# Splitting the returned columns of a feed-forward block two groups later, and starting its down projection with two units for one block of tokens

## The chip, the cores and the metric

The kernel runs on one core of one Trainium2 chip. The metric is device time in microseconds (us) of one execution. An execution with the hardware profiler on leaves a trace; times inside it are counted from the first instruction (its "span").

## The reference, cut to what matters

Two layers of a decoder trunk work on 256 tokens of width 1024. Each layer begins and ends with a feed-forward block, and the change touches only these (four of them in all):

```python
def swiglu(x, w_gu, w_down):                      # x 256 x 1024, w_gu 1024 x 5632, w_down 2816 x 1024
    gate, up = jnp.split(x @ w_gu, 2, axis=-1)
    return (jax.nn.silu(gate) * up) @ w_down
...
h = layer_norm(DEEPNORM_ALPHA * x + 0.5 * swiglu(x, ffn1_w_gu, ffn1_w_down), ln_g[0], ln_b[0])
... # three token mixers side by side, gated and projected, layer norm
return layer_norm(DEEPNORM_ALPHA * h + 0.5 * swiglu(h, ffn2_w_gu, ffn2_w_down), ln_g[2], ln_b[2])
```

## The kernel before, in words

**Weights.** All weights come as one stream of units of 128 x 1024 fp32 (512 KB). `unit` (L99) loads a unit into a buffer `raw` by a DMA from the SP queue (L110), and `split` (L115) makes two fp32r tiles of it: `whi`, a cast on ACT (L116), and `wlo`, the rest, a subtraction on DVE (L117). There are three `raw` buffers and five each of `whi` and `wlo`. Activations are split in the same way, by the same two lines. `mm3` (L131) multiplies two split operands with three matmuls (L126).

**Gate and up.** A feed-forward block has eleven groups (0 to 10) of 256 gate and 256 up columns. A group takes four units; for each of eight slices of the width and each of two blocks of 128 tokens (tb 0 and 1) three matmuls of 512 columns are issued, 48 in all. A group fills two of the four `acc` banks of PSUM, one per block. The loop is in `rest` (L357); group 0 is done by `first` or `both`.

**Out and back.** `out` (L330) takes a finished group. Per block ACT applies Silu from PSUM into a tile `t` (L336) and DVE multiplies by the up half (L337), which frees the bank. DVE transposes 32 x 32 squares, `t` into `z` (L340). Four DMAs from the POOL queue write `z` into a DRAM tile `tr` (L344), and a fifth brings it back in the order of a full transpose into `y` (L345). `t`, `z` and `y` share one tag of four buffers, `t2` (the trace calls all three `t`). Later `settle` (L348) splits `y` into `u0` to `u10` (lines 116 and 117 once more, `u<-t`), the operands of the down projection. Each call of `out` for group i first multiplies, then settles group i-1, then transposes group i.

**Down.** `projA` (L173) multiplies the 22 slices of `u` with 22 units. The sums of block 0 are two banks `a`, `b`, those of block 1 are `c`, `d` and a half bank `at` (`full_rows`, L216). `c` and `d` are the banks that group 10 used, so they are free only after its two multiplications on DVE. Unit 0 is done for block 0, then for block 1, then unit 1, and so on. After unit 8 the last group is settled (`along`). The last four or six units (`tail`) are kept to the end.

**What sets the order.** Each engine takes its instructions in one fixed order. A planner lays that order down when the program is built: on every engine it takes next what its own cost estimates say is ready, and of several ready ones the first in the program; loads and splits of weight units count as 300 instructions earlier than they stand (`AHEAD`, L100). `tc.issue_after(ins)` keeps what is traced inside it behind `ins`, but only on the engine of `ins`. In `settle` that is DVE, so the subtraction is held behind the multiplication of the newer group, and the cast on ACT is not held by anything but its operand.

Of the kernel before, what the change touches and what calls it, by code (L numbers as in the profile page):

```python
# [17 lines left out]
P = 128  # L18
D = 1024
# [3 lines left out]
NFT = FF // P  # L23
# [13 lines left out]

@with_exitstack
def tile_trunk(ctx, tc, x, xT, mem, memT_, wst, lnp, memln, cvw, rows, cst, out):
    nc = tc.nc  # L40
    pc = ctx.enter_context(tc.tile_pool(name="pc", bufs=1))
# [4 lines left out]
    p2 = ctx.enter_context(tc.tile_pool(name="p2", bufs=2))  # L46
# [7 lines left out]
    def nm(s):  # L54
        uid[0] += 1
        return f"{s}_{uid[0]}"

    def T(pool, shape, tag, dt=F32, bufs=None):
        kw = {} if bufs is None else {"bufs": bufs}
        return pool.tile(shape, dt, tag=tag, name=nm(tag), **kw)  # L60

    def acc():
        return T(psA, [P, 512], "acc")
# [30 lines left out]
        nc.scalar.copy(t.rearrange("p v k -> p (v k)"), zero.to_broadcast([P, 2 * S]))  # L94


    pos, newest = [0], [None]

    def unit(w=U, dst=None, cuts=1, behind=None):  # L99
        ahead = tc.high_priority(offset=AHEAD) if pos[0] >= 8 * P * U else nullcontext()  # L100
        raw = T(praw, [P, U], "raw")
        src = wst[pos[0]:pos[0] + P * w].rearrange("(p w) -> p w", p=P)
        pos[0] += P * w
        (ph, th), (pl, tl) = dst or ((phi, "whi"), (plo, "wlo"))
        with ahead:
            hi = T(ph, [P, U], th, F32R)
            lo = T(pl, [P, U], tl, F32R)
            for i in range(cuts):
                c = slice(i * w // cuts, (i + 1) * w // cuts)
                nc.sync.dma_start(raw[:, c], src[:, c])  # L110
                with tc.issue_after(behind) if behind else nullcontext():
                    newest[0] = split(hi[:, c], lo[:, c], raw[:, c])
        return hi, lo

    def split(hi, lo, src):  # L115
        nc.scalar.copy(hi, src)  # L116
        return nc.vector.tensor_tensor(lo, src, hi.bitcast(F32), op=ALU.subtract).ins  # L117
# [3 lines left out]
    def pe(ins):  # L121

        return tc.keep_in_program_order(ins) if pinned[0] else ins

    def matmul(*a, **k):
        return pe(nc.tensor.matmul(*a, **k))  # L126
# [4 lines left out]
    def mm3(o, l, r, first, last, skip=False):  # L131
        (lh, ll), (rh, rl) = l, r
        matmul(o, lh, rh, start=first, stop=False, skip_group_check=skip)
        matmul(o, lh, rl, start=False, stop=False, skip_group_check=skip)
        matmul(o, ll, rh, start=False, stop=last, skip_group_check=skip)

    def weave(work, steps):

# [34 lines left out]
    def projA(xt, w, kpu, nk, outs, tail=0, dsts=(), lead=0, after=None, behind=None, held=(), led=None, along=None):  # L173

        def one(k, kk, hi, lo, tb, j):
            ts = slice(tb * P, (tb + 1) * P)
            n = [o.shape[-1] for o in outs[tb]]
            c = kk * w + sum(n[:j])
            c = slice(c, c + n[j])
            mm3(outs[tb][j], (xt[0](k)[:, ts], xt[1](k)[:, ts]), (hi[:, c], lo[:, c]), k == 0, k == nk - 1)  # L180

        nu = nk // kpu
        units = {}

        def get(uu):
            if uu not in units:
                t = uu - (nu - tail)
                units[uu] = unit(kpu * w, dsts[t] if 0 <= t < len(dsts) else None, behind=behind if uu in held else None)
            return units[uu]

        def run(us, tb, js):
            for uu in us:
                for kk in range(kpu):
                    for j in js:
                        one(uu * kpu + kk, kk, *get(uu), tb, j)

        for tb in range(2):
            run(range(lead), tb, range(len(outs[tb])))
            if led:
                led(tb)  # L200
        for uu in range(lead, nu - tail):
            for tb in range(2):
                run([uu], tb, range(len(outs[tb])))
            if along and uu == 8:
                along(newest[0])
        for uu in range(nu - tail, nu):
            get(uu)
        turns = ()
        for tb in range(2):
            for j in range(len(outs[tb])):  # L210
                run(range(nu - tail, nu), tb, [j])
                if j and turns:
                    turns.pop(0)()
            turns = after and after(tb, outs)

    def full_rows():  # L216

        a, b, c, d = (acc() for _ in range(4))
        return [[a, b], [c, d[:, 0:S], at()[:, 0:S]]]
# [72 lines left out]
    class Ffn:  # L292
        def __init__(self, before=None):
            self.units = []
            for q in range(KD // 2):
                if before:
                    before(q)
                self.units.append(unit(cuts=2 if before and q == 0 else 1))
            self.hu, self.bank, self.due = {}, {}, None

        def h(self, i):
            if i not in self.hu:
# [17 lines left out]
        def both(self, hT):  # L320
            self.bank = {tb: acc() for tb in range(2)}
            for k in range(KD):
                hi, lo = self.units[k // 2]
                c = slice((k % 2) * 512, (k % 2) * 512 + 512)
                for tb in range(2):
                    ts = slice(tb * P, (tb + 1) * P)
                    mm3(self.bank[tb], (hT[0][:, k, ts], hT[1][:, k, ts]), (hi[:, c], lo[:, c]), k == 0, k == KD - 1)
            self.out(0, self.bank)

        def out(self, i, banks):  # L330


            t = T(p2, [P, 8, 2, 32], "t2", bufs=4)
            for tb in range(2):
                g, u = (banks[tb][:, c:c + S].rearrange("p (j x) -> p j x", j=8) for c in (0, S))
                nc.scalar.activation(t[:, :, tb, :], g, AF.Silu)  # L336
                ins = nc.vector.tensor_tensor(t[:, :, tb, :], t[:, :, tb, :], u, op=ALU.mult).ins  # L337
            self.settle(ins)
            z = T(p2, [P, 512], "t2", bufs=4)
            nc.vector.transpose(z, t.rearrange("p j t x -> p (j t x)"))  # L340
            y = T(p2, [P, 512], "t2", bufs=4)
            d = T(pd, [4, 32, 4, P], "tr")
            for q in range(4):
                nc.gpsimd.dma_start(d[:, :, q].rearrange("b c x -> c b x"), z[32 * q:32 * q + 32].rearrange("c (b x) -> c b x", b=4))  # L344
            nc.gpsimd.dma_start(y, d.rearrange("b c q x -> (b c) (q x)"))  # L345
            self.due = (i, y)

        def settle(self, behind):  # L348

            if self.due:  # L350
                (i, y), self.due = self.due, None
                hi, lo = (self.h(i)[:, n].rearrange("p a (t q s) -> p (a t) q s", t=2, q=4) for n in range(2))
                with tc.issue_after(behind):
                    split(hi, lo, y.rearrange("p (q n s) -> p n q s", q=4, n=4))
            self.last = behind

        def rest(self, hT, tail, dsts, post, mid={}, behind=None):  # L357
            for i in range(1, NFT // 2):
                banks = [acc() for _ in range(2)]
                for uu in range(KD // 2):  # L360
                    hi, lo = unit(behind=behind if i == 1 and uu < 2 else None)
                    for kk in range(2):
                        k, c = 2 * uu + kk, slice(kk * 512, kk * 512 + 512)
                        for tb in range(2):
                            ts = slice(tb * P, (tb + 1) * P)
                            mm3(banks[tb], (hT[0][:, k, ts], hT[1][:, k, ts]), (hi[:, c], lo[:, c]), k == 0, k == KD - 1)
                self.out(i, banks)
                for f in (2 * i, 2 * i + 1):
                    if f in mid:
                        with tc.issue_after(self.last):  # L370
                            mid[f]()
            outs = full_rows()
            projA((lambda k: self.hu[k // 2][:, 0, k % 2, :], lambda k: self.hu[k // 2][:, 1, k % 2, :]), D, 1, NFT, outs, tail, dsts, after=post, along=self.settle)

    class Post:

# [106 lines left out]
    def mixers(l, hT, mkT, mv_, post):  # L483
        xt = acc_of(hT)
        pinned[0] = True

        outs = [[acc()[:, :MOD // 2] for _ in range(2)] for _ in range(2)]
        projA(xt, MOD, 1, KD, outs, 3)
        ba = T(pu, [P, 2, 8], "ba")
        zs = T(pu, [P, 2, 512], "u3")  # L490
# [544 lines left out]
    for l in range(NL):  # L1035
# [4 lines left out]
        post = Post(lnp[l, 0, 0], lnp[l, 0, 1])  # L1040
# [9 lines left out]
        last = l == NL - 1  # L1050
        post = Post(lnp[l, 2, 0], lnp[l, 2, 1], last)
# [92 lines left out]
```

## Time and profile before

| what | value |
|---|---|
| three timed runs | 1354.88, 1358.7 and 1361.22 us, median 1358.7 us |
| the profiled execution | 1357.15 us, of which the span is 1355.4 us |
| matmuls, PE busy | 7160, 96% of the span |
| DVE, ACT, POOL busy | 62%, 48%, 15% of the span |
| DMA, mean over the span | 194 GB/s |
| granted TensorE clock, mean | 0.98 |

PE is TensorE's matmuls, PEld its weight loads, DVE is VectorE, ACT is ScalarE, POOL is GpSimd; SP issues the DMAs of the weight stream. Ends of matmuls are modelled, so neighbours overlap in the table of times and a PE that is "busy" need not be at its peak. In the views, `u<-t L116 ACT` is the cast of columns that came back, `u<-t,u L117 DVE` the subtraction, `t<-t L340` the transposition, `tr<-t L344` and `t<-tr L345` the way out to DRAM and back. A wait "A <- B: 10.0, 4, 3.0" says that A sat idle for 10.0 us before 4 of its instructions until B ended, 3.0 us at the longest. The two layers' feed-forward blocks lie at about 0 to 200, 490 to 690, 690 to 865 and 1155 to 1355 us.

### The profile page before, as it was taken

The page shows a single profiled execution, that of the slowest core. Times are in us where ns is not written, and L with a number is a line of the kernel's source. Part 1 is how long each engine was busy: PE and PEld are TensorE (multiplying, and loading weights), DVE is VectorE, ACT ScalarE, POOL GpSimd, SP SyncE. Part 2 cuts the span into 40 slices and gives each one's busy share as a digit, 9 for nine tenths or more (in the row PEclk, how much of TensorE's full clock was granted, in tenths as well). Part 3 has the DMA queues.
Part 4 walks back from the last instruction along what each step waited for, and adds up shares of the span by engine and source line. Part 5 has one row for each costly group of instructions (what it writes and reads, how often), then busy time and mean ns, then how long its engine had stood idle before and what let it go on. Part 6 is the DMA issues. An engine that isn't in the chain of part 4 may idle for free.

```text
span 1355.4 us, 19229 instructions
## 1 busy us (share of the span) xinstructions
PE 1294.4 (96%) x7160; PEld 1097.7 (81%) x7160; DVE 845.7 (62%) x1266; ACT 654.6 (48%) x979; POOL 197.8 (15%) x357
## 2 busy tenths in 40 slices
PE   8998799999999999998999989999999999999797
PEld 6876688999878788776888867899987788887686
DVE  5575557697556776455575554668867378654555
ACT  6443444566574544333444443446656644443441
POOL 0222200102301002121012220001024100121200
PEclk9998899999999999998999998999999999999899
DMA  8876774654644747666867666646554266666663
GB/s 266 290 241 198 244 235 144 203 182 135 155 137 136 233 131 226 218 207 190 261 206 242 209 213 214 215 147 211 172 138 147 91 189 199 196 207 219 219 200 110
DMA packets 77982, 263.54 MB, mean 194 GB/s; under 512 B 11872, under 2 KB 13024, under 8 KB 77888
## 3 DMA queue, kind: packets, MB, share of 16 engines
q1 hardware_dynamic: 66320, 232.53, 53.7%
q0 software_dynamic: 11568, 29.77, 7.6%
q8 instruction: 56, 0.92, 0.3%
q14 instruction: 38, 0.31, 0.1%
HBM read 247.45 MB, written 14.81 MB: 193 GB/s over the span
## 4 chain that ended last, share of the span: by engine, by line
PE 50%; DMA 27%; DVE 8%; issue 6%; ACT 6%; POOL 3%; SPq 0%; POOLq 0%; DVEq 0%; ACTq 0%
PE acc L126 40%; DMA t<-tr 9%; DMA raw<-in_wst_dram 9%; DMA tr<-t 9%; PE at L126 4%; DVE wlo L117 3%; POOL tr L344 3%; ACT whi L116 3%; PE sm L126 3%; ACT u L116 2%; DVE t L340 2%; PE sm L129 1%; DMA ms<-mst 1%; DVE u L117 1%; PE at L129 0%
## 5 line engine op out<-in xcount | busy, mean ns | idle before, releaser
L117 DVE TENSOR_TENSOR wlo<-raw,whi 128x1024 fp32r<-128x1024 f32 (+2 forms) x403 | 479.8, 1207 | 306.4 <-ACT whi L116 304.0
L116 ACT CAST whi<-raw 128x1024 fp32r<-128x1024 f32 (+2 forms) x403 | 409.2, 1034 | 404.8 <-DMA raw<-in_wst_dram 233.8
L126 PE MATMUL acc<-whi,hT 128*128 128x512 f32 (+1 forms) x1824 | 572.0, 391 | 15.1 <-ACT whi L116 15.1
L126 PEld LDWEIGHTS acc<-whi,hT 128*128 128x128 f32 x1824 | 345.2, 191 | 87.7 <-ACT whi L116 18.4
L126 PE MATMUL acc<-wlo,hT 128*128 128x512 f32 (+1 forms) x912 | 355.9, 390 | 8.9 <-DVE wlo L117 8.9
L126 PE MATMUL acc<-whi,u 128*128 128x512 f32 (+1 forms) x800 | 257.6, 386 | 24.0 <-DVE t L337 24.0
L126 PEld LDWEIGHTS acc<-wlo,hT 128*128 128x128 f32 x912 | 173.9, 191 | 46.7 <-DVE wlo L117 14.0
L126 PEld LDWEIGHTS acc<-whi,u 128*128 128x128 f32 x800 | 154.7, 195 | 57.2 <-DVE t L337 19.0
L344 POOL DMA_DIRECT2D tr<-t x176 | 96.2, 553 | 399.1 <-DVE t L340 385.6
L126 PE MATMUL acc<-wlo,u 128*128 128x512 f32 (+1 forms) x400 | 153.2, 383 | 0.0
L126 PE MATMUL acc<-hT,whi 128*128 128x256 f32 x672 | 122.3, 284 | 0.0
L126 PEld LDWEIGHTS acc<-hT,whi 128*128 128x128 f32 x672 | 104.7, 192 | 0.0
L117 DVE TENSOR_TENSOR u<-t,u 128x512 fp32r<-128x512 f32 x44 | 30.4, 692 | 113.7 <-ACT u L116 113.7
L116 ACT CAST u<-t 128x512 fp32r<-128x512 f32 x44 | 27.3, 620 | 144.8 <-DMA t<-tr 144.8
L126 PE MATMUL acc<-hT,wlo 128*128 128x256 f32 x336 | 95.1, 283 | 0.0
L126 PEld LDWEIGHTS acc<-wlo,u 128*128 128x128 f32 x400 | 78.2, 196 | 14.2 <-DVE wlo L117 0.3
L126 PEld LDWEIGHTS acc<-hT,wlo 128*128 128x128 f32 x336 | 64.4, 192 | 0.0
L345 POOL DMA_DIRECT2D t<-tr x44 | 24.6, 559 | 192.7 <-DMA tr<-t 140.0
L126 PE MATMUL at<-whi,u 128*128 128x256 f32 x152 | 39.8, 287 | 0.0
L337 DVE TENSOR_TENSOR t<-t,acc 128x256 f32<-128x256 f32 x88 | 36.0, 414 | 3.4 <-ACT t L336 3.3
L512 DVE SCALAR_TENSOR_TENSOR t<-acc,cw,t 128x255 f32<-128x255 f32 (+2 forms) x72 | 34.5, 479 | 0.9
L126 PE MATMUL acc<-whi,w 128*128 128x512 f32 (+1 forms) x96 | 31.0, 392 | 2.7 <-DVE w L117 2.7
(249 smaller groups left out, 1264.7 us busy)
## 6 DMA issues: line engine op xcount, KB each, us to landing
raw<-in_wst_dram SPq DMA_DIRECT2D x409, 512.0 KB, 4.4
tr<-t POOLq DMA_DIRECT2D x176, 64.0 KB, 3.9
t<-tr POOLq DMA_DIRECT2D x44, 256.0 KB, 3.5
raw<-in_wst_dram SPq DMA_DIRECT2D x16, 324.0 KB, 2.9
gB<-in_lnp_dram SPq DMA_DIRECT2D x6, 512.0 KB, 6.1
bB<-in_lnp_dram SPq DMA_DIRECT2D x6, 512.0 KB, 6.0
mdr<-w POOLq DMA_DIRECT2D x4, 512.0 KB, 6.8
w<-dr POOLq DMA_DIRECT2D x4, 512.0 KB, 12.3
```

Of the source, the lines that this page charges most:

```text
L116: nc.scalar.copy(hi, src)
L117: return nc.vector.tensor_tensor(lo, src, hi.bitcast(F32), op=ALU.subtract).ins
L126: return pe(nc.tensor.matmul(*a, **k))
L129: return pe(nc.tensor.transpose(*a))
L337: ins = nc.vector.tensor_tensor(t[:, :, tb, :], t[:, :, tb, :], u, op=ALU.mult).ins
L340: nc.vector.transpose(z, t.rearrange("p j t x -> p (j t x)"))
L344: nc.gpsimd.dma_start(d[:, :, q].rearrange("b c x -> c b x"), z[32 * q:32 * q + 32].rearrange("c (b x) -> c b x", b=4))
L345: nc.gpsimd.dma_start(y, d.rearrange("b c q x -> (b c) (q x)"))
L512: nc.vector.scalar_tensor_tensor(yc[:, j, d:], b[:, j, :S - d], w[:, t:t + 1], yc[:, j, d:], op0=ALU.mult, op1=ALU.add)
```

## The change

Settling is put off: `out` keeps a list of groups that are on their way, and when it has transposed group i it settles group i-2, if there is one, with the subtraction held behind the transposition instead of the multiplication. `y` moves to a tag with two buffers, `pt`, which the feed-forward blocks did not use. Two groups are left for the down projection, settled after its units 2 and 5; what is handed to `issue_after` there is now a matmul, an instruction of PE, so it holds nothing on ACT or DVE. And the down projection begins with `lead` 2: units 0 and 1 for block 0, then units 0 and 1 for block 1, then the others as before.

```diff
     def unit(w=U, dst=None, cuts=1, behind=None):
...
                 with tc.issue_after(behind) if behind else nullcontext():
-                    newest[0] = split(hi[:, c], lo[:, c], raw[:, c])
+                    split(hi[:, c], lo[:, c], raw[:, c])
...
     def mm3(o, l, r, first, last, skip=False):
...
-        matmul(o, ll, rh, start=False, stop=last, skip_group_check=skip)
+        return matmul(o, ll, rh, start=False, stop=last, skip_group_check=skip).ins
...
         for tb in range(2):
-            run(range(lead), tb, range(len(outs[tb])))
+            if lead:
+                run(range(lead), tb, range(len(outs[tb])))
             if led:
                 led(tb)
         for uu in range(lead, nu - tail):
             for tb in range(2):
-                run([uu], tb, range(len(outs[tb])))
-            if along and uu == 8:
-                along(newest[0])
+                ins = run([uu], tb, range(len(outs[tb])))
+            if along and uu in (2, 5):
+                along(ins)
...
-            self.hu, self.bank, self.due = {}, {}, None
+            self.hu, self.bank, self.due = {}, {}, []
...
                 ins = nc.vector.tensor_tensor(t[:, :, tb, :], t[:, :, tb, :], u, op=ALU.mult).ins
-            self.settle(ins)
+            self.last = ins
             z = T(p2, [P, 512], "t2", bufs=4)
-            nc.vector.transpose(z, t.rearrange("p j t x -> p (j t x)"))
-            y = T(p2, [P, 512], "t2", bufs=4)
+            ins = nc.vector.transpose(z, t.rearrange("p j t x -> p (j t x)")).ins
+            if len(self.due) > 1:
+                self.settle(ins)
+            y = T(p2, [P, D], "pt")[:, 0:512]
...
-            self.due = (i, y)
+            self.due.append((i, y))
...
             if self.due:
-                (i, y), self.due = self.due, None
+                i, y = self.due.pop(0)
                 hi, lo = (self.h(i)[:, n].rearrange("p a (t q s) -> p (a t) q s", t=2, q=4) for n in range(2))
                 with tc.issue_after(behind):
                     split(hi, lo, y.rearrange("p (q n s) -> p n q s", q=4, n=4))
-            self.last = behind
...
-            projA(..., D, 1, NFT, outs, tail, dsts, after=post, along=self.settle)
+            projA(..., D, 1, NFT, outs, tail, dsts, 2, post, along=self.settle)
```

More of the change, by code (lines that the diff above doesn't have):

```diff
@@ L94, in tile_trunk @@
         nc.scalar.copy(t.rearrange("p v k -> p (v k)"), zero.to_broadcast([P, 2 * S]))
-    pos, newest = [0], [None]
+    pos = [0]
     def unit(w=U, dst=None, cuts=1, behind=None):
@@ L179, in one @@
             c = slice(c, c + n[j])
-            mm3(outs[tb][j], (xt[0](k)[:, ts], xt[1](k)[:, ts]), (hi[:, c], lo[:, c]), k == 0, k == nk - 1)
+            return mm3(outs[tb][j], (xt[0](k)[:, ts], xt[1](k)[:, ts]), (hi[:, c], lo[:, c]), k == 0, k == nk - 1)
         nu = nk // kpu
@@ L191, in run @@
         def run(us, tb, js):
+            ins = None
             for uu in us:
@@ L194, in run @@
                     for j in js:
-                        one(uu * kpu + kk, kk, *get(uu), tb, j)
+                        ins = one(uu * kpu + kk, kk, *get(uu), tb, j)
+            return ins
         for tb in range(2):
-            run(range(lead), tb, range(len(outs[tb])))
+            if lead:
+                run(range(lead), tb, range(len(outs[tb])))
             if led:
@@ L372, in rest @@
             outs = full_rows()
-            projA((lambda k: self.hu[k // 2][:, 0, k % 2, :], lambda k: self.hu[k // 2][:, 1, k % 2, :]), D, 1, NFT, outs, tail, dsts, after=post, along=self.settle)
+            projA((lambda k: self.hu[k // 2][:, 0, k % 2, :], lambda k: self.hu[k // 2][:, 1, k % 2, :]), D, 1, NFT, outs, tail, dsts, 2, post, along=self.settle)
     class Post:
```

## The prediction

> **What bounds the kernel now.** I read the page first, then the waits, then the busy time by stretch, then the timeline of one group on each engine.
>
> ```profile
> span 1355.4 us, 19229 instructions
> ...
> PE 50%; DMA 27%; DVE 8%; issue 6%; ACT 6%; POOL 3%; SPq 0%; POOLq 0%; DVEq 0%; ACTq 0%
> PE acc L126 40%; DMA t<-tr 9%; DMA raw<-in_wst_dram 9%; DMA tr<-t 9%; PE at L126 4%; DVE wlo L117 3%; POOL tr L344 3%; ACT whi L116 3%; PE sm L126 3%; ACT u L116 2%; DVE t L340 2%; PE sm L129 1%; DMA ms<-mst 1%; DVE u L117 1%; PE at L129 0%
> ```
>
> The chain that ended last is half PE, but 18% of it is the way of the columns to DRAM and back, in a kernel whose PE looks 96% busy. The waits say who stands still for that way:
>
> ```profile
> ACT u L116 <- DMA t<-tr: 144.8, 43, 7.0
> ...
> DVE u L117 <- ACT u L116: 120.8, 49, 6.4
> ```
>
> All but one of the 44 casts wait for their columns, 3.4 us each (144.8 / 43), and DVE stands behind them. One turn of it, in layer 1's first block, groups 9 and 10, first ACT, then DVE, then POOL:
>
> ```profile
> 808.61 0.62 ACT L116 CAST u<-t 128x512 fp32r<-128x512 f32 x1 [2.88 <-DMA t<-tr]
> 809.14 2.96 ACT L116 CAST whi<-raw 128x1024 fp32r<-128x1024 f32 x3
> 812.00 0.38 ACT L336 ACTIVATE t<-acc 128x256 f32<-128x256 f32 x1
> 816.06 1.04 ACT L116 CAST whi<-raw 128x1024 fp32r<-128x1024 f32 x1 [3.69 <-DMA raw<-in_wst_dram]
> 817.01 0.38 ACT L336 ACTIVATE t<-acc 128x256 f32<-128x256 f32 x1
> 820.26 0.62 ACT L116 CAST u<-t 128x512 fp32r<-128x512 f32 x1 [2.87 <-DMA t<-tr]
> ```
>
> ```profile
> 809.87 0.71 DVE L340 STREAM_TRANSPOSE t<-t 128x512 f32<-128x512 f32 x1
> ...
> 813.87 0.41 DVE L337 TENSOR_TENSOR t<-t,acc 128x256 f32<-128x256 f32 x1
> 817.14 1.23 DVE L117 TENSOR_TENSOR wlo<-raw,whi 128x1024 fp32r<-128x1024 f32 x1 [2.85 <-ACT whi L116]
> 818.28 0.41 DVE L337 TENSOR_TENSOR t<-t,acc 128x256 f32<-128x256 f32 x1
> 820.91 0.69 DVE L117 TENSOR_TENSOR u<-t,u 128x512 fp32r<-128x512 f32 x1 [2.21 <-ACT u L116]
> 821.52 0.71 DVE L340 STREAM_TRANSPOSE t<-t 128x512 f32<-128x512 f32 x1
> ```
>
> ```profile
> 810.87 2.26 POOL L344 DMA_DIRECT2D tr<-t  x4 [4.63 <-DVE t L340]
> 817.07 0.56 POOL L345 DMA_DIRECT2D t<-tr  x1 [3.94 <-DMA tr<-t]
> ```
>
> This is a closed ring. The transposition at 809.87 sends columns out; they are back for the cast at 820.26, 10.4 us later; the subtraction follows at 820.91, and only behind it in DVE's order comes the next transposition, at 821.52. One turn takes 11.65 us, with nothing of PE in it. Group 10 had both multiplications done at 818.7, so its transposition could have gone 2.8 us earlier.
>
> How long a turn lasts on average is in the first and last start of the transposition, eleven groups in each of the four blocks:
>
> ```profile
> L340 DVE STREAM_TRANSPOSE t<-t x11: 703/705/714, 22.5 to 154.0; 128x512 f32<-128x512 f32 x11
> ...
> L340 DVE STREAM_TRANSPOSE t<-t x11: 702/705/712, 499.1 to 628.2; 128x512 f32<-128x512 f32 x11
> ...
> L340 DVE STREAM_TRANSPOSE t<-t x11: 702/705/715, 700.3 to 821.5; 128x512 f32<-128x512 f32 x11
> ...
> L340 DVE STREAM_TRANSPOSE t<-t x11: 702/705/712, 1164.8 to 1289.5; 128x512 f32<-128x512 f32 x11
> ```
>
> Divided by ten turns: 13.2, 12.9, 12.1 and 12.5 us, 12.7 on average; the DMAs are on average 1 us slower than in the turn shown. What PE needs, and what it loses, is in the table by stretch (gate and up, then the start of the down projection, for each block; last an undisturbed stretch):
>
> ```profile
> 26.00:140.00 114.00, 105.43 (x441) 84.49 (x441) 68.93 (x106) 52.78 (x72) 24.36 (x45) 0.97 0.77 246
> 140.00:160.00 20.00, 11.57 (x47) 8.90 (x46) 10.32 (x13) 7.67 (x12) 6.58 (x12) 0.83 0.79 260
> 490.00:612.00 122.00, 117.43 (x506) 95.38 (x505) 64.90 (x78) 51.06 (x69) 24.70 (x45) 0.99 0.67 213
> 612.00:626.00 14.00, 8.54 (x31) 6.41 (x30) 6.58 (x8) 5.07 (x7) 2.74 (x5) 0.76 0.66 206
> 690.00:808.00 118.00, 116.33 (x507) 95.35 (x506) 66.97 (x81) 52.99 (x71) 24.61 (x45) 0.99 0.69 219
> 808.00:823.00 15.00, 10.03 (x33) 7.57 (x32) 8.67 (x11) 6.66 (x9) 3.22 (x6) 0.66 0.66 214
> 1155.00:1278.00 123.00, 118.80 (x513) 96.86 (x512) 66.48 (x81) 53.71 (x73) 24.71 (x45) 0.99 0.68 214
> 1278.00:1292.00 14.00, 8.86 (x29) 6.90 (x29) 8.07 (x10) 5.71 (x8) 4.25 (x8) 0.63 0.61 193
> 12.00:60.00 48.00, 48.00 (x213) 39.75 (x212) 30.44 (x36) 27.33 (x34) 7.98 (x15) 1.00 0.88 281
> ```
>
> The columns are the length, then busy time of PE, PEld, DVE, ACT and POOL, the granted clock, DMA share and GB/s. From 12 to 60 PE does 213 matmuls in 48 us, 0.225 us each, so a group of 48 takes it 10.8 us. The ring needs 12.7. The difference is first soaked up (PE runs ahead, on weights already split) and then paid where PE needs a bank that the late engines have not emptied:
>
> ```profile
> 809.12 0.39 PE L126 MATMUL acc<-whi,u 128*128 128x512 f32 x1
> ...
> 810.25 0.39 PE L126 MATMUL acc<-whi,u 128*128 128x512 f32 x1
> 814.34 0.80 PE L126 MATMUL acc<-whi,u 128*128 128x512 f32 x1 [3.70 <-DVE t L337]
> 814.93 0.63 PE L126 MATMUL acc<-wlo,u 128*128 128x512 f32 x1
> 815.36 0.63 PE L126 MATMUL acc<-whi,u 128*128 128x512 f32 x1
> ...
> 818.75 0.58 PE L126 MATMUL acc<-whi,u 128*128 128x256 f32 x1 [1.27 <-DVE t L337]
> ```
>
> PE starts the down projection at 809.12, runs through block 0's share of unit 0, and then waits for the multiplications that free banks c and d, at 813.87 and 818.28. After the pause its matmuls start 0.43 us apart instead of 0.225, and the clock of that stretch is 0.66.
>
> **What there is to gain.** Idle PE in gate and up (length less busy): 8.6 + 4.6 + 1.7 + 4.2 = 19 us. Clock not granted there: 3% of 114 and 1% of 122, 118 and 123, together 7 us. At the start of the down projections: 8.4 + 5.5 + 5.0 + 5.1 = 24 us idle, and 17% of 20, 24% of 14, 34% of 15 and 37% of 14, together 17 us of clock, of which I count 12, since what falls into the pauses costs nothing. In all 19 + 7 + 24 + 12 = 62 us.
>
> **The later settling.** The transposition of group i no longer stands behind the subtraction of group i-1 on DVE, and the ring is open. The multiplication of group 10 then trails PE only by ACT's and DVE's own work: Silu 0.38, a weight cast 1.05, Silu 0.38, multiplication 0.41, with handovers 2.5 us. ACT's work per group is 4 x 1.05 + 2 x 0.38 + 0.62 = 5.6 us and DVE's 4 x 1.23 + 2 x 0.41 + 0.71 + 0.69 = 7.1 us, both under 10.8, so PE sets the pace. In the order of before, the cast of group i-1 stands right behind the second Silu of group i. Its columns would be back 10.4 us after a transposition that starts 2.5 us behind PE's end of group i-1, which is 2.5 + 10.4 - 10.8 = 2.1 us after PE's end of group i, about when ACT gets there; with the average DMA it waits 1 us, which its 5.2 us of slack cover. If that cover is gone, weight casts come late, with five split units (13.5 us of PE work) still ahead. I leave 8 us of the 26 in gate and up, most of it in the first block, where the memory's normalisation takes DVE and POOL time: gain 18 us, between 8 and 24.
>
> The cast is not held later by anything in the change; only its place in the program moves. The subtraction of group i-2 now follows the transposition on DVE, 0.69 us ahead of weight subtractions that it stood ahead of before too: nothing. New is that the return DMA of group i waits for the subtraction of group i-2, because `y` has two buffers; that ends 1.4 us after the transposition starts, and the return is issued 7.2 us after it (809.87 to 817.07), so nothing queued behind it on POOL is late. The five DMAs of a group are the same. The weight stream must go faster: 4 x 0.52 MB of weights and twice 0.26 MB of columns in 10.8 us is 243 GB/s; the stretch from 12 to 60 moved 281 with PE never idle, so that is no new bound.
>
> **The last two groups.** Settled after units 2 and 5 and held by nothing, their subtractions may be put where DVE waits for the DMA, some 3 us (as with the casts now) each. Unit work of PE for five split units covers it; uncovered it is 2 x 3 x 4 = 24 us, which I take at nothing, 4 us at most. The slices are not used before unit 18.
>
> **Two units for block 0.** Unit 1's six matmuls for block 0 move ahead of block 1: 6 x 0.225 = 1.35 us more before bank c is needed, 2.7 in all, and c's own three give 0.7 more before d. Against a multiplication at 2.5 us that is cover; against one 4 to 8 us late, after a slow DMA, it is not. I leave 10 of the 36 us: gain 26, between 14 and 32. [...]
>
> **Sum.** 1357.15 - 18 - 26 = 1313 us, with the bounds 1301 to 1335. The median of the three runs lies 1.5 us above the profiled execution, less than the sum is good for.
>
> **Rivals.** *The cast is put ahead of the second Silu (slower).* ACT's order for the changed program is not in this profile. The transposition now comes 0.69 us earlier behind its group, so by the planner's own reckoning columns return earlier, and the cast may be taken as soon as they are, between the two Silus. Then the second Silu, its multiplication and the transposition wait for the previous group's DMA: the ring closes again, through ACT, and longer. 10.4 + cast 0.62 + weight cast 1.04 + its subtraction 1.23 + multiplication 0.41 + handovers 0.1 = 13.8 us a turn, 2.15 more than 11.65. Over 4 x 10 turns that is 86 us, less 5 from the first two units: 1438 us. It decides from about half of the groups on; with fewer, a turn of 13.8 and one of PE's pace average below 12.7. For it speaks that the cast is tied to nothing; against it, that in the rows above a weight cast and a Silu fit between the first Silu and the cast. [...]
>
> *The cast alternates (no change).* If it stands ahead of the second Silu in every other group, two turns need 13.8 + about 9 (three weight casts, the wait for the fourth's data at 816.06, two Silus) = 22.8, 11.4 on average, plus the 1 us of the average DMA 12.4: the old pace. What is left is block 0's 1.35 us in each block, 5 us: 1352 us, between 1343 and 1362. The same comes out if the change does not do what it says because the split stays tied to the DMA on DVE.
>
> **How the numbers follow.** The ring opens: 0.57, at 1313. Alternating: 0.23. Closed through ACT in half or more of the groups: 0.20, from 1362 to 1438. About 0.5% (6.8 us) is what a measurement of this kernel can tell from no change. Faster is the forecast and a part of the alternating case, 0.57 + 0.05; the same 0.16; slower 0.20 and a remainder of the alternating one, 0.22. The range is to hold 0.8: the forecast's own, widened to 1292 because the 8 and 10 us left over may be less and the clock's share more, and upward through the alternating case to 1366. The forecast's own range is 1301 to 1335.
>
> **What would show it.** Right: transpositions 10.8 to 11.2 us apart; casts of returned columns waiting 1 us or less each; the wait of PE for the multiplication, L337, nearly gone and the clock of the down projections' first 15 us above 0.9. The forecast is wrong if the mean turn stays above 12 us. For the slower rival: `u<-t` between the two Silus on ACT, the second Silu behind a wait for `t<-tr`, turns of 13.8 us. If turns shorten but PE still waits at the down projection, the cover there was mis-sized.

## The result, and the profile after

The changed kernel takes 1315.96 us (median of four runs, 1306.78 to 1318.15) against 1359.96 us for the kernel before, timed beside it (four runs, 1354.88 to 1364.73): a ratio of 0.966 over all runs (0.968 of the medians), 95% interval 0.960 to 0.972. The profiled execution took 1317.82 us. The forecast was 1313.

The page's span and the chain that ended last:

```profile
span 1315.8 us, 19159 instructions
...
PE 73%; DMA 13%; DVE 5%; ACT 5%; issue 3%; POOL 1%; SPq 0%; DVEq 0%; ACTq 0%; POOLq 0%
PE acc L126 62%; DMA raw<-in_wst_dram 8%; PE at L126 4%; DMA pt<-tr 3%; ACT whi L116 3%; PE sm L126 3%; DVE wlo L117 2%; DMA tr<-t 2%; PE sm L129 1%; DMA ms<-mst 1%; PE acc L321 1%; PE acc L318 1%; PE acc L319 1%; PE at L129 0%; POOL tr L349 0%
```

PE's share of the chain rises from 50 to 73%, and the way of the columns (`tr<-t` with `pt<-tr`, since `y` is now called `pt`) falls from 18 to 5%. The lines have moved: Silu is L339, the multiplication L340, the transposition L343, the DMAs out L349, the DMA back L350. The waits:

```profile
ACT u L116 <- DMA pt<-tr: 105.5, 37, 7.1
...
DVE u L117 <- ACT u L116: 30.6, 17, 5.9
...
PE acc L126 <- DVE t L340: 9.2, 5, 4.3
```

The last of these read, in the kernel before:

```profile
PE acc L126 <- DVE t L337: 24.0, 9, 6.4
```

DVE stands behind the casts for 30.6 us instead of 120.8, PE waits 9.2 us for the multiplication instead of 24.0. But ACT still waits 105.5 us for the columns, 2.9 us in each of 37 casts. The way of the columns is as long as it was: from the start of the transposition to the landing of the return DMA it takes 11.9 us on average over the 44 groups, and took 11.8 before. What has changed is that the next transposition no longer stands behind it. First and last transposition of each block:

```profile
L343 DVE STREAM_TRANSPOSE t<-t x11: 695/711/712, 23.7 to 152.8; 128x512 f32<-128x512 f32 x11
...
L343 DVE STREAM_TRANSPOSE t<-t x11: 705/711/712, 499.7 to 614.0; 128x512 f32<-128x512 f32 x11
...
L343 DVE STREAM_TRANSPOSE t<-t x11: 705/711/712, 685.3 to 797.0; 128x512 f32<-128x512 f32 x11
...
L343 DVE STREAM_TRANSPOSE t<-t x11: 705/712/715, 1136.8 to 1249.4; 128x512 f32<-128x512 f32 x11
```

The four stretches are 129.1, 114.3, 111.7 and 112.6 us long, where they were 131.5, 129.1, 121.2 and 124.7. They are shorter by 2.4, 14.8, 9.5 and 12.1 us, together 38.8 of the 39.6 us by which the span is shorter. What lies between them differs by 1.8 us or less, save for 3.5 us less between blocks 3 and 4, where block 3's last transposition comes 3.2 us late (below). The first block gives almost nothing. The same by stretch (columns as in the prediction: gate and up, then the start of the down projection, for each block):

```profile
26.00:138.00 112.00, 104.77 (x441) 84.85 (x440) 68.80 (x105) 52.16 (x72) 25.40 (x46) 0.95 0.83 254
138.00:160.00 22.00, 15.41 (x57) 11.64 (x56) 11.68 (x15) 9.48 (x14) 6.61 (x12) 0.77 0.71 238
470.00:600.00 130.00, 128.75 (x593) 107.05 (x592) 85.72 (x116) 62.05 (x82) 24.70 (x45) 1.00 0.69 220
600.00:620.00 20.00, 20.00 (x104) 17.10 (x103) 10.11 (x12) 6.69 (x9) 4.91 (x9) 1.00 0.62 176
660.00:786.00 126.00, 124.97 (x574) 103.47 (x573) 84.94 (x114) 61.46 (x81) 28.93 (x53) 1.00 0.73 239
786.00:800.00 14.00, 14.00 (x72) 11.92 (x71) 8.08 (x10) 6.45 (x9) 2.60 (x5) 1.00 0.60 184
1112.00:1239.00 127.00, 126.89 (x585) 105.74 (x584) 82.11 (x111) 58.13 (x78) 26.30 (x48) 1.00 0.67 215
1239.00:1253.00 14.00, 11.40 (x50) 9.44 (x49) 8.74 (x11) 7.40 (x10) 3.32 (x7) 0.88 0.67 209
```

In blocks 2 and 3 PE is without a gap at the start of the down projection, at full clock. Block 1 keeps 7.2 us of idle PE in gate and up and 6.6 at its down projection, block 4 one pause of 2.6 us.

One turn on DVE in block 3, groups 9 and 10 (weight subtractions left out):

```profile
782.29 0.71 DVE L343 STREAM_TRANSPOSE t<-t 128x512 f32<-128x512 f32 x1
782.92 0.65 DVE L117 TENSOR_TENSOR u<-pt,u 128x512 fp32r<-128x512 f32 x1
...
792.72 0.41 DVE L340 TENSOR_TENSOR t<-t,acc 128x256 f32<-128x256 f32 x1
796.35 0.69 DVE L117 TENSOR_TENSOR u<-pt,u 128x512 fp32r<-128x512 f32 x1 [3.21 <-ACT u L116]
796.95 0.70 DVE L343 STREAM_TRANSPOSE t<-t 128x512 f32<-128x512 f32 x1
```

The subtraction at 782.92 has its operand ready and waits for nothing. Group 10's last multiplication ends at 793.13, 2.8 us behind PE, which began the down projection at 790.29. The one at 796.35 is a left-over group that nothing holds: the planner put it ahead of group 10's transposition, and DVE waited 3.21 us there, with PE fully busy in that stretch.

### The profile page after: what moved, and what is told of

It reads as the page before. It is cut to its first block, busy times and chain, and to the rows that moved or that the text cites. A ratio compares the mean times of both kernels' runs of the same rounds, so it can differ in the third digit from the quotient of the medians.

```text
span 1315.8 us, 19159 instructions
## 1 busy us (share of the span) xinstructions
PE 1279.6 (97%) x7160; PEld 1091.7 (83%) x7160; DVE 849.7 (65%) x1266; ACT 658.9 (50%) x979; POOL 197.8 (15%) x357
## 4 chain that ended last, share of the span: by engine, by line
PE 73%; DMA 13%; DVE 5%; ACT 5%; issue 3%; POOL 1%; SPq 0%; DVEq 0%; ACTq 0%; POOLq 0%
PE acc L126 62%; DMA raw<-in_wst_dram 8%; PE at L126 4%; DMA pt<-tr 3%; ACT whi L116 3%; PE sm L126 3%; DVE wlo L117 2%; DMA tr<-t 2%; PE sm L129 1%; DMA ms<-mst 1%; PE acc L321 1%; PE acc L318 1%; PE acc L319 1%; PE at L129 0%; POOL tr L349 0%
## 5 line engine op out<-in xcount | busy, mean ns | idle before, releaser
L126 PEld LDWEIGHTS acc<-whi,hT 128*128 128x128 f32 x1824 | 343.2, 190 | 80.4 <-ACT whi L116 11.8
L126 PE MATMUL acc<-whi,u 128*128 128x512 f32 (+1 forms) x800 | 253.0, 380 | 9.2 <-DVE t L340 9.2
L349 POOL DMA_DIRECT2D tr<-t x176 | 96.2, 553 | 387.9 <-DVE t L343 374.8
L116 ACT CAST u<-pt 128x512 fp32r<-128x512 f32 x44 | 27.3, 620 | 105.5 <-DMA pt<-tr 105.5
L350 POOL DMA_DIRECT2D pt<-tr x44 | 24.6, 558 | 156.3 <-DMA tr<-t 83.4
L117 DVE TENSOR_TENSOR u<-pt,u 128x512 fp32r<-128x512 f32 x44 | 29.0, 660 | 22.7 <-ACT u L116 22.7
L340 DVE TENSOR_TENSOR t<-t,acc 128x256 f32<-128x256 f32 x88 | 36.3, 416 | 4.6 <-ACT t L339 3.5
L339 ACT ACTIVATE t<-acc 128x256 f32<-128x256 f32 x88 | 32.6, 376 | 10.6 <-PE acc L126 10.3
```

## The experiments

**Theory**: the gain is the opened ring, DVE's order alone. **Rivals**: the two units for block 0 bring a good part; the distance of two groups is needed; ACT's wait of 105 us is the next bound. The first four kernels ran on one chip, beside 13 runs of the kernel before (median 1359.05 us).

### Later settling without the two units

```diff
-            projA(..., D, 1, NFT, outs, tail, dsts, 2, post, along=self.settle)
+            projA(..., D, 1, NFT, outs, tail, dsts, 0, post, along=self.settle)
```

> The later settling alone: the changed kernel, but the down projection begins as before (unit 0 for both blocks of tokens). If the gain comes from opening the ring on DVE (the theory), transpositions stay 10.4 to 11.2 us apart in the last three blocks, and what is lost against the changed kernel is 1.35 us of cover in each of four blocks and the clock after those pauses: 1322 to 1330 us. If the two units at the start of the down projection were the main part (rival), the time stays above 1340 us.

Measured: 1311.77 us (1311.22 to 1315.11), ratio 0.965 (0.962 to 0.969). That is no loss against the changed kernel, where 6 to 14 us were expected, so the two units bring nothing that this timing sees. The starts of the down projections in blocks 2 to 4, by stretch:

```profile
600.00:620.00 20.00, 20.00 (x108) 17.05 (x108) 8.07 (x9) 6.04 (x8) 3.29 (x6) 1.00 0.66 197
...
780.00:800.00 20.00, 19.85 (x100) 16.57 (x99) 12.10 (x13) 10.12 (x12) 4.61 (x9) 1.00 0.75 231
...
1233.00:1250.00 17.00, 15.98 (x80) 13.24 (x79) 10.55 (x12) 9.08 (x11) 4.59 (x9) 1.00 0.77 241
```

PE is idle for 1.2 us in all three together, where the kernel before lost 5.5 + 5.0 + 5.1 = 15.6: the order of before already covers nearly all that is left of the multiplication's lateness.

### The two units alone

```diff
-            projA(..., D, 1, NFT, outs, tail, dsts, after=post, along=self.settle)
+            projA(..., D, 1, NFT, outs, tail, dsts, 2, post, along=self.settle)
```

> The two units for block 0 alone, on the kernel before, with its settling as it was. The theory: the multiplications that free the banks still come 4 and 9 us behind PE, so 1.35 us more cover in each block gives about 5 us, 1350 to 1356 us, and the mean turn stays at 12.5 us or more. The rival (the start of the down projection is most of the gain): 1335 us or less.

Measured: 1358.93 us, ratio 0.9999 (0.9975 to 1.0023): no effect, a miss even of the small one expected. PE at block 3's down projection, then DVE:

```profile
814.58 0.39 PE L126 MATMUL acc<-whi,u 128*128 128x512 f32 x1
...
817.31 0.50 PE L126 MATMUL acc<-wlo,u 128*128 128x512 f32 x1 [0.97 <-DVE wlo L117]
...
819.91 0.50 PE L126 MATMUL acc<-whi,u 128*128 128x512 f32 x1 [1.19 <-DVE t L337]
...
824.07 0.38 PE L126 MATMUL acc<-whi,u 128*128 128x256 f32 x1 [3.20 <-DVE t L337]
```

```profile
814.84 0.69 DVE L117 TENSOR_TENSOR u<-t,u 128x512 fp32r<-128x512 f32 x1 [2.35 <-ACT u L116]
815.45 0.70 DVE L340 STREAM_TRANSPOSE t<-t 128x512 f32<-128x512 f32 x1
816.07 3.45 DVE L117 TENSOR_TENSOR wlo<-raw,whi 128x1024 fp32r<-128x1024 f32 x3
819.44 0.41 DVE L337 TENSOR_TENSOR t<-t,acc 128x256 f32<-128x256 f32 x1
...
823.61 0.41 DVE L337 TENSOR_TENSOR t<-t,acc 128x256 f32<-128x256 f32 x1
```

The multiplications come 4.9 and 9.0 us behind PE's start at 814.58, since DVE is still in the closed ring. Against that stand 12 + 3 = 15 matmuls of cover, 3.4 us. But the kernel before had already had most of it: its trace shows, between the two pauses, block 1's three of bank `c`, three halves into `at` and two of unit 1 (814.34 to 816.85), 6 + 3 + 1.5 + 2 = 12.5 in all. And one of the new ones was itself late: unit 1's `wlo` was not there at 817.31. The pauses here add up to 0.97 + 1.19 + 3.20 = 5.4 us, and to 3.70 + 1.27 = 5.0 in the kernel before: the cover shifts idle time from the first wait to the second. By operation and tiles, the orders of DVE, ACT and POOL are those of the kernel before.

### One line moved, and nothing else

The kernel before, with group i-1 still settled with group i, but behind its transposition:

```diff
-            self.settle(ins)
             z = T(p2, [P, 512], "t2", bufs=4)
-            nc.vector.transpose(z, t.rearrange("p j t x -> p (j t x)"))
+            self.settle(nc.vector.transpose(z, t.rearrange("p j t x -> p (j t x)")).ins)
+            self.last = ins
```

> On the kernel before, one line is moved: group i-1 is still settled in the turn of group i, but behind the transposition of group i instead of ahead of it. Nothing is put off by two groups, the buffers and the down projection are as before. If it is DVE's order alone that closes the ring (theory), the columns are back about when the transposition is done, DVE waits about 1 us a turn within its slack, and the time is near the settling alone: 1322 to 1336 us. If two groups of distance are needed (rival), DVE's weight subtractions now stand behind the wait for the DMA and the time stays above 1345 us.

Measured: 1313.0 us (1312.03 to 1313.78), ratio 0.966 (0.963 to 0.969). That is better than the 1322 to 1336 expected: the whole gain of the changed kernel is in the place of one instruction on one queue, and neither the second group of distance nor the second buffer is needed for it. Nothing else moved with it where the gain is made: compared by operation and tiles, the two traces have the same order on PE throughout; in blocks 2 to 4 they differ in 30 places, all on DVE, and in each the transposition has changed places with the subtraction of returned columns. (In block 1 a few more instructions changed places on DVE, and one each on ACT and POOL.) Waits, and the transpositions of blocks 2 to 4:

```profile
ACT u L116 <- DMA t<-tr: 86.8, 40, 6.2
...
DVE u L117 <- ACT u L116: 39.0, 35, 2.1
```

```profile
L339 DVE STREAM_TRANSPOSE t<-t x11: 705/711/714, 499.5 to 607.8; 128x512 f32<-128x512 f32 x11
...
L339 DVE STREAM_TRANSPOSE t<-t x11: 704/711/715, 683.7 to 792.9; 128x512 f32<-128x512 f32 x11
...
L339 DVE STREAM_TRANSPOSE t<-t x11: 706/711/712, 1136.7 to 1244.6; 128x512 f32<-128x512 f32 x11
```

10.8, 10.9 and 10.8 us a turn, PE's own pace. DVE still waits for the cast in 35 places, 1.1 us each, but behind the transposition, and with PE at its own pace this wait lies in DVE's slack.

### The slower rival, built by hand

The changed kernel, with the cast of group i-1 held on ACT between the two Silus of group i:

```diff
+                if tb:
+                    cast = self.cast(silu)
-                nc.scalar.activation(t[:, :, tb, :], g, AF.Silu)
+                with tc.issue_after(cast) if tb and cast else nullcontext():
+                    silu = nc.scalar.activation(t[:, :, tb, :], g, AF.Silu).ins
```

> The changed kernel with the cast of group i-1 on ACT held between the two Silus of group i (a weight cast stands between the first Silu and it); the subtraction on DVE stays two groups late, behind the transposition. Theory of the ring: it is closed again through ACT, 10.4 us from a transposition to the return of its columns, then cast 0.62, second Silu 0.38, multiplication 0.41 and handovers 0.3, 12.1 us a turn with fast DMAs and 13.1 with average ones, against 11.65 and 12.7 before. The gain is gone: 1350 to 1375 us. If the subtraction on DVE alone mattered (rival), the place of the cast changes little and the time stays within 10 us of 1316.

Measured: 1387.7 us (1384.75 to 1392.39), ratio 1.021 (1.017 to 1.025), slower clear of the noise. The direction is right, the size is above what was expected. ACT in block 3 (the cast is L368 there, Silu L342):

```profile
771.26 0.39 ACT L342 ACTIVATE t<-acc 128x256 f32<-128x256 f32 x1
776.78 1.05 ACT L116 CAST whi<-raw 128x1024 fp32r<-128x1024 f32 x1 [5.14 <-DMA raw<-in_wst_dram]
780.43 0.62 ACT L368 CAST u<-pt 128x512 fp32r<-128x512 f32 x1 [2.59 <-DMA pt<-tr]
780.96 0.38 ACT L342 ACTIVATE t<-acc 128x256 f32<-128x256 f32 x1
```

The cast waits for its DMA, the second Silu behind it, and with it the multiplication that frees the bank. PE's wait for the multiplication is 62.8 us in 25 places, against 9.2 in 5. The mean turns of the four blocks are 14.9, 13.0, 12.5 and 13.0 us, and 40 of the 44 casts stand between two Silus of one group; in the changed kernel none does. Raw weights are late in the same place (5.14 us ahead of the weight cast at 776.78), as they were in the kernel before (3.69 at 816.06). The kernel before had the same DMA in its ring, but there only the transposition waited for it, not a bank of PE.

### The changed kernel again, and the cast really two groups later

In the changed kernel ACT's order is that of before: the cast stands right behind the second Silu of the next group, since `issue_after` held DVE's half only. Here ACT's half is held as well, behind the second Silu two groups on, and the last two groups behind the splits of newer weight units:

```diff
-            if along and uu in (2, 5):
-                along(ins)
+            if along and uu in (4, 10):
+                along(*newest[0])
...
-        def settle(self, behind):
+        def settle(self, act, behind):
...
-                with tc.issue_after(behind):
+                with tc.issue_after(act), tc.issue_after(behind):
```

These two and the kernel of the next heading ran on one chip, beside nine runs of the kernel before (1358.94 us).

> The changed kernel itself, beside the two below on one chip. By its own four runs 1316 us (1307 to 1318). If the two units for block 0 cost something, it is over 1313 by more than the intervals; if they bring or cost nothing, it agrees with the 1312 and 1313 of the two kernels that leave them out, within 4 us.

> The changed kernel with ACT's half of the split, the cast, really two groups later as well: in its program order it stands behind the second Silu of two groups on, so that it no longer waits for its DMA; the last two are held behind splits of later weight units. In the changed kernel ACT waits 105 us in all at these casts (37 waits). Theory, the wait lies in ACT's slack and PE sets the pace: turns stay at 10.8 to 11 us, the wait goes to under 20 us and the time only by what the last pause of block 4 (2.8 us) and the late last transpositions cost: 1309 to 1317 us. Rival, ACT's wait is the new bound behind DVE's: 20 us or more off, under 1296 us.

Measured: the changed kernel 1311.2 us (1308.85 to 1316.81), ratio 0.965 (0.962 to 0.967), the same as without the two units (0.965) and with one line moved (0.966). With the cast later: 1303.42 us (1302.46 to 1306.82), ratio 0.959 (0.957 to 0.961), 7.8 us less. That lies between the theory's range (1309 to 1317) and the rival's (under 1296), nearer to the theory's: neither forecast it. ACT's wait did go:

```profile
ACT u L116 <- DMA pt<-tr: 11.3, 4, 5.1
```

The first transpositions of blocks 1 to 4 are at 22.8, 498.1, 681.8 and 1134.3 us in the changed kernel's second trace and at 22.0, 489.9, 673.6 and 1125.9 in this one, and the spans end at 1309.3 and 1300.7. The difference is 0.8 us at the start of block 1, 8.2 at that of block 2, and 8.6 at the end: it is made in block 1 and nowhere else. (Block 1's last transposition, at 151.7 and 143.6, has it already.) So in blocks 2 to 4 ACT's slack takes the whole wait, and in block 1 it does not. Up to 96 us PE is never idle in either, and does 328 matmuls in both. Block 1 by stretch, the changed kernel first:

```profile
96.00:138.00 42.00, 36.22 (x133) 27.56 (x132) 23.18 (x25) 19.30 (x28) 9.67 (x19) 0.84 0.72 203
138.00:160.00 22.00, 16.19 (x67) 12.38 (x66) 12.76 (x16) 9.69 (x15) 7.11 (x13) 0.84 0.73 235
```

```profile
22.00:96.00 74.00, 74.00 (x328) 61.32 (x327) 50.30 (x86) 37.79 (x48) 18.96 (x34) 1.00 0.91 288
96.00:138.00 42.00, 36.22 (x152) 27.46 (x150) 27.35 (x31) 22.42 (x33) 11.58 (x21) 1.00 0.79 238
138.00:160.00 22.00, 17.43 (x85) 14.72 (x86) 11.12 (x13) 9.04 (x11) 3.30 (x6) 0.84 0.77 249
```

From 96 to 138 PE is busy for 36.22 us in both, but with 133 matmuls in one and 152 in the other: the clock is 0.84 against 1.00. The 19 matmuls more are some 4 us of the gain (19 x 0.225 us); the 18 more from 138 to 160, of which some are half as wide, are most of the rest. What the traces show of the clock behind a pause is in the last section.

### What is left in block 1

The kernel with one line moved, and the return of the memory's means and deviations (the normalisation that runs beside block 1) issued from POOL behind the next group's four column DMAs:

```diff
-            nc.gpsimd.dma_start(got["row"], d.rearrange("a t p -> (a t p)").partition_broadcast(P))
+            got["d"] = d
+
+        def row():
+            got["row"] = T(pu, [P, D], "gB")[:, 0:512]
+            nc.gpsimd.dma_start(got["row"], got["d"].rearrange("a t p -> (a t p)").partition_broadcast(P))
...
-        return ... {8: vecs, 10: rows_, 13: halves_, 15: lambda: half(0), 17: lambda: half(1), 19: keep}
+        return ... {8: vecs, 10: rows_, 12: row, 13: halves_, 15: lambda: half(0), 17: lambda: half(1), 19: keep}
```

> The kernel before with the one line moved (the split settled behind the next transposition on DVE, 1313 us) and one further edit: in block 1 the return of the memory's means and deviations, issued from POOL, is put behind the next group's four column DMAs instead of ahead of the fourth, which stood 9.7 us behind its wait. Theory, the rest of block 1's loss (7.5 us idle and 12% of the clock from 96 to 138, 7.6 us idle from 138 to 160) hangs on that late group: 3 to 12 us less, 1301 to 1310. Rival, block 1 loses by the raw weights that come late (DMA engines busy 80 to 82% there): no difference, 1311 to 1315.

Measured: 1310.79 us (1310.19 to 1313.01), ratio 0.964 (0.962 to 0.966) against 0.966 (0.963 to 0.969) without the edit: no difference. The columns' return DMA is issued at 108.25 us instead of 114.84, but the transposition at 113.1 still stands 18.3 us behind the one before it, and ACT waits 4.7 us for raw weights at 103.9 and 3.1 at 108.4. That speaks for the rival, but does not show it.

The last kernel takes the one with the later cast and moves the memory's work two groups forward, so that SP and POOL wait less for it. (It moves from groups 4 and 5 to 2 and 3; the expectation counts each one too low.) It ran beside eleven runs of the kernel before, median 1360.72 us.

```diff
-        return ... {8: vecs, 10: rows_, 13: halves_, 15: lambda: half(0), 17: lambda: half(1), 19: keep}
+        return ... {4: vecs, 6: rows_, 13: halves_, 15: lambda: half(0), 17: lambda: half(1), 19: keep}
```

> The kernel with the cast two groups later (1303.4 us) and one more edit: in block 1 the memory's rows are loaded behind group 1 instead of 3 and their means and deviations taken behind group 2 instead of 4, so that the SP queue no longer waits for DVE before it loads the memory's columns (two waits ahead of weight loads at 83 and 85 us) and the wait for the means on POOL (9.4 us at 103) stands between two groups, not within one. Theory, what block 1 still loses (5.8 us idle from 96 to 138 and 4.6 from 138 to 160) hangs on those two queues, with the group at 110 us, 18.5 us behind the one before: that turn goes to 13 us or less and the time to 1294 to 1300. Rival, block 1 loses by the memory's own work on DVE and ACT, or by DMA bandwidth (79% busy): the long turn only moves, 1301 to 1306.

Measured: 1302.46 us (1300.41 to 1302.77), ratio 0.956 (0.953 to 0.960), against 1303.42 and 0.959 (0.957 to 0.961): at most a few us, within the intervals. The long turn of 18.5 us becomes two, 15.9 and 16.5 us, at 61 and 98 us. It only moves, as the rival said. What block 1 still loses is not settled: memory work on DVE and ACT and late raw weights go together there, and the DMAs are near the highest rates that these traces show over tens of us: 278 GB/s from 96 to 138 in this kernel, 288 from 22 to 96 in the one before it, 297 in one slice of 33 us on the page of the changed kernel.

## Why the prediction was right, point by point

**The bound was read rightly.** The ring through DVE's order set the pace of blocks 2 to 4, and the one-line kernel shows it alone: 10.8 to 10.9 us a turn there, against the 10.8 that PE needs. Block 1's turn of 13.2 us hung on more than the ring: it is 13.0 in the one-line kernel. Of "what there is to gain", 62 us, the profile before to the profile after gave 39.3 and the medians 44.0; forecast were 44.

**The later settling, gain 18 in gate and up.** By the same count (length less busy, and the missing clock) gate and up still lose 7.2 + 1.3 + 1.0 + 0.1 = 9.6 us of idle and 5% of 112, 5.6 us of clock: 15 of 26, so the gain is 11, not 18, inside the bounds of 8 and 24 but at their low end. The 8 us to be left "most of it in the first block" are 15, 12.8 of them there.

**The cast's wait.** "With the average DMA it waits 1 us" failed: it waits 2.9 us in 37 groups. Part of it is the term 10.4 us, read from one fast turn, where the 44 groups of the changed kernel take 11.9 on average; the rest of the difference stays open. That ACT's slack covers it is right for blocks 2 to 4 and wrong for block 1, where it costs 7 to 8 us: the kernel with the later cast shows both. "The cast is not held later by anything in the change" was right, and is what this kernel mends.

**Two units for block 0, gain 26 at the down projections.** The size came out (24 us idle became 6.6 + 0 + 0 + 2.6 = 9.2, and 17 us of clock became 23% of 22 and 12% of 14, 6.7), but by luck, since the reason given in that paragraph failed. The two units bring nothing alone, and taking them away costs nothing. With the ring open, in block 3 group 10's multiplication ends 2.8 us behind PE's start of the down projection (2.5 were reckoned), and 12.5 matmuls of cover, 2.8 us, were there before. The prediction's count of cover left out that PE's old order also had `at` and two matmuls of unit 1 between banks `c` and `d`: the rows of PE quoted there leave out those between 815.36 and 818.75, and they were not counted. What was gained there belongs to the settling, which gives all of the gain by itself. So the sum came out at 1313 with one term too high and the other put down to the wrong half of the change. (The stretches of the two traces differ in extent; by them the two terms come to 33 to 36 of the 39.3 us, by the transpositions to 38.8.)

**The last two groups, taken at nothing.** Right in the blocks looked at: a floating subtraction made DVE wait 3.21 us at 796 ahead of the last transposition, with no PE time lost there.

**Block 4's pause.** In the profiled execution ACT was late by one column wait of 3.55 us and then one weight wait of 2.86, and PE paused 2.60 us; the second trace of the same kernel has no such pause.

**The rival on the other side.** Its mechanism is real, a ring closed through ACT: 1387.7 us when built, within the 1362 to 1438 given for it, with turns of 12.5 to 14.9 us for 13.8. It did not come about because the planner left the casts where they were: none of the 44 stands between the two Silus of a group (in block 3 the second Silu is at 780.56 and the cast behind it, at 782.03). The alternating case had the same condition and fell with it.

**What would show it.** Transpositions 10.8 to 11.2 us apart: 11.4, 11.2 and 11.3 in blocks 2 to 4 with the late last one, 12.9 in block 1, 11.7 on average. Casts that wait 1 us or less: not so, 2.9. PE's wait nearly gone: 9.2 of 24.0 left. Clock above 0.9 in the down projections: 1.00, 1.00, 0.88 and, in block 1, 0.77.

## What to carry to other kernels

When an engine waits for a far transfer, ask first what stands behind the waiting instruction on its queue: here a wait of 87 to 105 us could stay on ACT, and moving one instruction on DVE behind the work that others need gave all of the gain; taking ACT's wait away as well was worth 7.8 us more, all in block 1. Before adding cover for a late engine, count in the trace every matmul that already stands in the gap, and find out why the engine is late. Here an order constraint held only the engine of the instruction that it named: with the subtraction held on DVE, the casts on ACT waited 105.5 us for the columns, and 11.3 us once ACT's half was held too.

## What the runs showed of the hardware

What a pause of PE costs in clock does not go by its length alone in these traces. In those of the kernel before and of the changed kernel the granted clock is 1.00 or 0.50, and the stretches at half clock, apart from the one at the end of the program, are 3.41, 6.83 or 10.24 us long, nine and four of them. Within each of the two traces they start a whole number of 3.41 us apart, and the windows shown here are of that length. Block 4 of the changed kernel, with its pause of 2.60 us from 1245.3 to 1247.9:

```profile
1243.99:1247.41 3.42, 1.31 (x6) 0.75 (x4) 1.17 (x2) 1.33 (x2) 0.00 (x0) 1.00 0.90 246
1247.41:1250.82 3.41, 2.92 (x10) 2.63 (x11) 2.44 (x6) 1.66 (x2) 0.40 (x1) 0.50 0.82 304
1250.82:1254.23 3.41, 3.41 (x23) 3.04 (x22) 2.30 (x2) 1.05 (x1) 1.78 (x4) 1.00 0.55 132
```

PE is idle for 62% of the first window (1.31 us busy of 3.42), and the next one is at half clock. In the changed kernel's second trace a window with 1.77 us of idle PE (1.64 busy of 3.41) is followed by four at half clock, 13.66 us. In the last of the four PE is busy throughout, and the clock behind it is 1.00:

```profile
107.45:110.86 3.41, 1.64 (x7) 0.82 (x5) 0.48 (x1) 1.33 (x2) 0.40 (x1) 1.00 1.01 375
110.86:114.28 3.42, 2.67 (x7) 2.16 (x7) 2.92 (x4) 0.00 (x0) 0.56 (x1) 0.50 0.65 193
...
121.10:124.52 3.42, 3.42 (x10) 2.65 (x9) 2.46 (x3) 3.17 (x6) 0.19 (x1) 0.50 0.77 235
124.52:127.93 3.41, 3.41 (x16) 2.81 (x15) 2.85 (x5) 3.41 (x6) 1.10 (x2) 1.00 0.79 240
```

In the kernel without the two units PE is idle for 1.69 us of one window and for 1.23 us of the next, 2.92 us in all, and both are at full clock:

```profile
103.87:107.29 3.42, 1.73 (x8) 1.11 (x6) 0.00 (x0) 0.62 (x1) 1.10 (x2) 1.00 0.88 277
107.29:110.70 3.41, 2.18 (x8) 1.58 (x9) 2.48 (x3) 0.71 (x2) 0.08 (x1) 1.00 0.70 208
```

In the one-line kernel PE is idle for 1.16 of the 2 us from 791 to 793, and the clock is 1.00 there and up to 797. In the kernel before, the longest pause between 587.49 and 590.90 us is 1.57 us, PE is busy for 1.32 of those 3.41 us, and the clock is 0.50 from 590.90 to 594.31.

Counted over the traces of the kernel before and of the changed kernel from 12 us on, without the end of the program: 13 windows at full clock stand ahead of one at half clock. PE is idle for 57 to 94% of 12 of them and for 48% of the other (785.47 to 788.88 in the kernel before). Of the windows at full clock with another behind them, the one with the most idle PE has 56% (113.04 to 116.46 there). Behind a window at half clock the clock was full again where PE had been idle for 14% or less of it, and stayed at half where it had been idle for 23% or more. (Ends of matmuls are modelled, so these shares are not sharp.) That is how the windows of two traces lie; what sets the clock was not tested. Block 1 of the changed kernel's second trace and of the kernel with the later cast, both with 36.22 us busy of 42, came to clocks of 0.84 and 1.00. That the later cast spreads its idle time more evenly over the windows would fit these counts, but is not shown here.
